# Operands of the fp32r matmuls moved by 32 bytes in SBUF, with padded weight buffers

## The chip, the cores and the metric

The kernel runs on one core of one Trainium2 chip. The metric is the device time of one execution in microseconds (us). A matmul has a stationary operand, which a weight load brings into TensorE (PE) ahead of it, and a moving operand, which streams past it column by column; both are read from SBUF.

## The reference

One layer of a hybrid trunk over 256 frames of width 2048, in float32. All heavy work is two products with large weights:

```python
h = rmsnorm(x, norm_w)
proj = h @ w_in                      # (256, 2048) @ (2048, 13344)
z, xbc, dt_raw, q, k, v, g = jnp.split(proj, IN_SPLITS, axis=-1)
# state-space group: conv, SiLU, chunked scan, gate, group norm    -> y_ssd (256, 2048)
# stick-breaking attention, 16 heads of 128, gate                  -> y_sba (256, 2048)
mix = jnp.concatenate([y_ssd, y_sba], axis=-1)
return x + mix @ w_out               # (256, 4096) @ (4096, 2048), then a final rmsnorm
```

## The kernel before, in words

Both products run in fp32r, with each factor cut into a high and a low part, and three of the four part products are kept. Activations are cut once: `hT` holds the input's high and low parts (128 partitions, 16 slices k of the depth, 2 parts, 256 frames), and `mix_s_hi`, `mix_s_lo`, `mix_a_hi`, `mix_a_lo` hold those of the two head groups. Weights stream through: `load` (L208) brings 1 MB into one of four `raw` buffers, and `cut` (L210) makes the parts `hi` (ScalarE, L225) and `lo` (VectorE, L228) of half of that, in buffers of 1,024 columns, three of each.

The weights' columns are worked off in blocks, one after another, by `run_blocks`, in an order written out by hand. There are two kinds:

- "feat" blocks, 37 of them with 256 columns (in the tiles c, b, z, x, q, k, g): the weights are stationary, the activations move. For each of 16 slices k, L262 issues two matmuls in which all 512 columns of `hT[:, k]` (high and low part, which lie side by side) move past `hi`, and L265 two in which the 256 columns of its high part move past `lo`.
- "tok" blocks (z0 to z2, c1, v0 to v3, o0 to o3): the activations are stationary, 128 frames at a time, and 512 columns of `hi` or `lo` move (288 in c1). For each slice and each half of the frames there are three matmuls, L256 to L258; o3's last step takes 256 columns at a time (L239 to L241).

By the code that is 37 x 64 = 2,368 fp32r matmuls in feat blocks, half with 512 and half with 256 columns, and 288 + 96 + 384 + 774 = 1,542 in tok blocks, 3,910 in all. Besides them, transposes (moving operand `ident`) and small float32 products of the scan and the attention are put between the steps of the blocks by queues with costs; each of those float32 products runs as two passes in the trace, a transpose as one.

SBUF is laid out by pools in the order of their creation: `const`, `stream` (raw, hi, lo), `mixp` (xt and mix_s_hi, sz and mix_s_lo), then `qv`, `half`, `hpool` (hT), `ssd`, and later `mixa`, `att` and, for o3, `fin` (further hi and lo buffers). Places are multiples of 32 bytes. Before the change, raw, hi, lo, xt, sz, mix, the tok tiles of q, k, v and g, hT and nearly all of the rest start 32 bytes past a multiple of 64 bytes in their partition: the first hi buffer at byte 57,632, hT at 133,408, mix_s_hi at 82,208. All slices that the fp32r matmuls take are multiples of 512 bytes (1,152 in c1) from there. `ident`, `ones` and `tri`, the first tiles of `const`, start at multiples of 64.

Of the kernel before, what the change touches and what calls it, by code (L numbers as in the profile page):

```python
# [9 lines left out]
F32 = mybir.dt.float32  # L10
F32R = mybir.dt.float32r
# [7 lines left out]
P = 128  # L19
# [33 lines left out]
def hybrid_kernel(ctx, tc, x, norm_w, w_in, conv_w, conv_b, dt_bias, a_log, d_skip,  # L53
# [9 lines left out]
    const = ctx.enter_context(tc.tile_pool(name="const", bufs=1))  # L63
# [7 lines left out]
        return ps_s.tile([P, 512], F32, tag="s", name=name)  # L71


    ident = const.tile([P, P], F32, name="ident")
    make_identity(nc, ident)
    ones = const.tile([P, P], F32, name="ones")
# [133 lines left out]
    def cut(b, s, each=None):  # L210

        n, name, width = b["n"], f"{b['name']}_{s}", KS[b["kind"]]
        k, kc = s * width, KC[b["kind"]]
        src = raws[b["name"], k // kc][:, k % kc:k % kc + width, :]
        pool, bufs = (b["pool"](), 3) if b["pool"] is not None and s % 2 else (stream, 3)

        def part(which):
            t = pool.tile([P, 1024], F32R, tag=which, name=f"{which}_{name}", bufs=bufs)
            return t[:, 0:width * n].rearrange("p (k n) -> p k n", k=width)
        hi, lo = part("hi"), part("lo")  # L220
        parts = [slice(0, width)] if each is None else [slice(i, i + 1) for i in range(width)]
        for ks in parts:
            if each is not None:
                each(ks.start)
            ins = ac.copy(hi[:, ks, :], src[:, ks, :])  # L225
            if b is blocks[0]:
                last_cut[0] = ins.ins
            ve.tensor_tensor(out=lo[:, ks, :], in0=src[:, ks, :], in1=hi[:, ks, :].bitcast(F32), op=ALU.subtract)  # L228
        cuts[b["name"], s] = hi, lo
# [820 lines left out]
```

## Time and profile before

| what | value |
|---|---|
| median of 3 runs | 829.27 us (829.16 to 829.34) |
| the profiled execution | 829.74 us |
| its span, first to last instruction | 828.0 us |
| PE busy | 814.8 us, 98% |
| VectorE busy, ScalarE busy | 529.8 us (64%), 453.8 us (55%) |
| granted TensorE clock, mean | 0.998 |

Matmuls are pipelined, so a matmul's own duration in the trace overlaps its successor's. What a matmul costs in a stream is the distance from its start to the start of the next one. The timeline view gives starts to 0.01 us, and the distance is taken over many of them.

### The profile page before, as it was taken

The numbers are of one execution on the slowest core, as the hardware profiler recorded it, in microseconds if no ns is written. First come the engines' busy times: TensorE is split into PE (matmuls) and PEld (weight loads), VectorE is DVE, ScalarE is ACT, GpSimd is POOL, SyncE is SP. The second block draws the span as 40 slices with busy tenths as digits, with TensorE's granted clock in tenths as the row PEclk, the third lists the DMA queues.
The fourth block names the chain that finished last, engine by engine and source line by source line (L and its number), as shares of the span: only waits on it lengthen the run. The fifth ranks groups of instructions, "written<-read, shape, count | busy, mean of one in ns | idle before, by whom it ended". The sixth has DMA issues, their size and how long they took to land.

```text
span 828.0 us, 11381 instructions
## 1 busy us (share of the span) xinstructions
PE 814.8 (98%) x4411; PEld 697.5 (84%) x4411; DVE 529.8 (64%) x754; ACT 453.8 (55%) x666; POOL 67.1 (8%) x133
## 2 busy tenths in 40 slices
PE   8999999999999999999999999999999999999995
PEld 6888988888888888888888888888888888888884
DVE  5669596577899868686545654566545655454543
ACT  5766578955797745365445444455444544344433
POOL 0000003000201011022001210022000310000000
PEclk9999999999999999999999999999999999999999
DMA  9854677566667665545566645665465846555712
GB/s 297 289 183 137 193 221 221 179 198 186 200 187 216 196 221 157 171 144 191 156 192 174 187 156 162 197 197 160 153 203 189 320 153 200 181 185 196 254 52 101
DMA packets 117114, 156.34 MB, mean 189 GB/s; under 512 B 3356, under 2 KB 83764, under 8 KB 116676
## 3 DMA queue, kind: packets, MB, share of 16 engines
q1 hardware_dynamic: 115316, 149.29, 57.2%
q0 software_dynamic: 1712, 6.33, 2.3%
q8 instruction: 34, 0.56, 0.3%
q14 instruction: 20, 0.16, 0.1%
q10 hardware_dynamic: 32, 0.01, 0.0%
HBM read 153.48 MB, written 2.13 MB: 188 GB/s over the span
## 4 chain that ended last, share of the span: by engine, by line
PE 97%; DMA 1%; ACT 1%; DVE 1%; SPq 0%; issue 0%; DVEq 0%
PE mm_x L262 7%; PE mm_q L262 7%; PE mm_g L262 7%; PE mm_k L262 7%; PE mm_o L256 7%; PE mm_o L258 7%; PE mm_o L257 7%; PE mm_q L265 4%; PE mm_k L265 4%; PE mm_x L265 4%; PE mm_g L265 4%; PE mm_v L256 4%; PE mm_v L257 3%; PE mm_v L258 3%; PE mm_z L257 3%; PE mm_z L256 3%
## 5 line engine op out<-in xcount | busy, mean ns | idle before, releaser
L228 DVE TENSOR_TENSOR lo_o<-raw_o,hi_o 128x1024 fp32r<-128x1024 f32 x64 | 78.1, 1224 | 74.4 <-ACT hi_o L225 74.4
L225 ACT CAST hi_o<-raw_o 128x1024 fp32r<-128x1024 f32 x64 | 67.1, 1053 | 95.3 <-PE mm_o L258 81.6
L262 PE MATMUL mm_q<-hT,hi_q 128*128 128x512 f32 x256 | 82.5, 403 | 0.0
L262 PE MATMUL mm_k<-hT,hi_k 128*128 128x512 f32 x256 | 81.6, 400 | 0.0
L262 PE MATMUL mm_x<-hT,hi_x 128*128 128x512 f32 x256 | 80.9, 397 | 0.0
L262 PE MATMUL mm_g<-hT,hi_g 128*128 128x512 f32 x256 | 80.6, 396 | 0.0
L228 DVE TENSOR_TENSOR lo_v<-raw_v,hi_v 128x1024 fp32r<-128x1024 f32 x32 | 39.2, 1225 | 44.2 <-ACT hi_v L225 44.2
L228 DVE TENSOR_TENSOR lo_g<-raw_g,hi_g 128x1024 fp32r<-128x1024 f32 x32 | 39.2, 1225 | 38.1 <-ACT hi_g L225 38.1
L225 ACT CAST hi_v<-raw_v 128x1024 fp32r<-128x1024 f32 x32 | 33.6, 1051 | 47.5 <-PE mm_v L258 27.8
L225 ACT CAST hi_g<-raw_g 128x1024 fp32r<-128x1024 f32 x32 | 33.6, 1051 | 44.6 <-PE mm_g L262 25.9
L265 PEld LDWEIGHTS mm_x<-hT,lo_x 128*128 128x128 f32 x256 | 48.1, 188 | 11.3
L265 PEld LDWEIGHTS mm_k<-hT,lo_k 128*128 128x128 f32 x256 | 48.1, 188 | 11.4
L265 PEld LDWEIGHTS mm_g<-hT,lo_g 128*128 128x128 f32 x256 | 48.1, 188 | 11.3
L265 PEld LDWEIGHTS mm_q<-hT,lo_q 128*128 128x128 f32 x256 | 48.0, 188 | 11.2
L225 ACT CAST hi_q<-raw_q 128x1024 fp32r<-128x1024 f32 x32 | 33.5, 1048 | 39.6 <-PE mm_q L262 18.1
L228 DVE TENSOR_TENSOR lo_k<-raw_k,hi_k 128x1024 fp32r<-128x1024 f32 x32 | 39.7, 1241 | 22.7 <-ACT hi_k L225 22.7
L228 DVE TENSOR_TENSOR lo_x<-raw_x,hi_x 128x1024 fp32r<-128x1024 f32 x32 | 39.8, 1244 | 22.2 <-ACT hi_x L225 17.3
L228 DVE TENSOR_TENSOR lo_q<-raw_q,hi_q 128x1024 fp32r<-128x1024 f32 x32 | 39.1, 1223 | 19.0 <-ACT hi_q L225 18.9
L265 PE MATMUL mm_q<-hT,lo_q 128*128 128x256 f32 x256 | 50.9, 280 | 0.0
L228 DVE TENSOR_TENSOR lo_z<-raw_z,hi_z 128x1024 fp32r<-128x1024 f32 (+1 forms) x34 | 39.3, 1160 | 17.9 <-ACT hi_z L225 17.7
L256 PE MATMUL mm_o<-hi_o,mix_s_hi 128*128 128x512 f32 x128 | 50.6, 395 | 0.0
L265 PE MATMUL mm_k<-hT,lo_k 128*128 128x256 f32 x256 | 50.4, 278 | 0.0
(263 smaller groups left out, 1985.3 us busy)
## 6 DMA issues: line engine op xcount, KB each, us to landing
raw_o<-in_w_out_dram SPq DMA_DIRECT2D x32, 1024.0 KB, 5.2
raw_x<-in_w_in_dram SPq DMA_DIRECT2D x16, 1024.0 KB, 5.3
raw_q<-in_w_in_dram SPq DMA_DIRECT2D x16, 1024.0 KB, 5.3
raw_k<-in_w_in_dram SPq DMA_DIRECT2D x16, 1024.0 KB, 5.3
raw_v<-in_w_in_dram SPq DMA_DIRECT2D x16, 1024.0 KB, 5.0
raw_g<-in_w_in_dram SPq DMA_DIRECT2D x16, 1024.0 KB, 5.3
raw_z<-in_w_in_dram SPq DMA_DIRECT2D x12, 1024.0 KB, 5.3
raw_b<-in_w_in_dram SPq DMA_DIRECT2D x4, 1024.0 KB, 5.5
```

The source lines that it names most:

```text
L225: ins = ac.copy(hi[:, ks, :], src[:, ks, :])
L228: ve.tensor_tensor(out=lo[:, ks, :], in0=src[:, ks, :], in1=hi[:, ks, :].bitcast(F32), op=ALU.subtract)
L256: te.matmul(o, lhsT=ah[:, ts], rhs=hi[:, k2, :], start=first, stop=False)
L257: te.matmul(o, lhsT=ah[:, ts], rhs=lo[:, k2, :], start=False, stop=False)
L258: te.matmul(o, lhsT=al[:, ts], rhs=hi[:, k2, :], start=False, stop=last)
L262: te.matmul(acc[i], lhsT=hi[:, k2, i * P:(i + 1) * P], rhs=hT[:, k, :, :].rearrange("p a s -> p (a s)"), start=first, stop=False, skip_gro ...
L265: te.matmul(acc[i][:, 0:SEQ], lhsT=lo[:, k2, i * P:(i + 1) * P], rhs=hT_hi[:, k, :], start=False, stop=last, skip_group_check=True)
```

## The change

A tile of 8 columns (32 bytes) that nothing uses is put first into `const`, so that everything behind it starts 32 bytes later. The buffers of hi and lo are 1,040 columns wide in place of 1,024, and feat blocks use columns 8 to 1,031 of theirs, tok blocks columns 0 to 1,023 as before.

```diff
+    const.tile([P, 8], F32, name="pad")
     ident = const.tile([P, P], F32, name="ident")
...
         def part(which):
-            t = pool.tile([P, 1024], F32R, tag=which, name=f"{which}_{name}", bufs=bufs)
-            return t[:, 0:width * n].rearrange("p (k n) -> p k n", k=width)
+            t = pool.tile([P, 1040], F32R, tag=which, name=f"{which}_{name}", bufs=bufs)
+            at = 8 if b["kind"] == "feat" else 0
+            return t[:, at:at + width * n].rearrange("p (k n) -> p k n", k=width)
```

Worked out from the sizes, raw, hT, mix and the buffers of hi and lo then start at multiples of 64 bytes (a buffer is 4,160 bytes, 65 x 64), the weights of feat blocks 32 bytes past one, and so do `ident`, `ones` and `tri`. No instruction is added, removed or reordered.

## Rows read from the trace of the kernel before

**Rows 1.** The page: busy time of PE; granted clock over 40 slices.
```profile
PE 814.8 (98%) x4411; PEld 697.5 (84%) x4411; DVE 529.8 (64%) x754; ACT 453.8 (55%) x666; POOL 67.1 (8%) x133
...
PEclk9999999999999999999999999999999999999999
```
**Rows 2.** The page: share of engines in the chain that ended last.
```profile
PE 97%; DMA 1%; ACT 1%; DVE 1%; SPq 0%; issue 0%; DVEq 0%
```
**Rows 3.** Waits of PE: who waited for whom, us in total, times, longest.
```profile
PE warm L319 <- POOL ident masks.py:199: 1.5, 1, 1.5
PE ps_x L403 <- DMA xt<-in_x_dram: 1.2, 2, 0.6
PE ps_q L743 <- DVE ssq L738: 0.9, 1, 0.9
PE ps_w L856 <- issue: 0.8, 1, 0.8
PE mm_z L257 <- DVE lo_z L228: 0.2, 1, 0.2
```
**Rows 4.** Timeline of PE (start, us, instruction), tok block, 512 columns: first, last of 14.
```profile
699.82 0.39 PE L256 MATMUL mm_o<-hi_o,mix_s_hi 128*128 128x512 f32 x1
...
702.99 0.39 PE L258 MATMUL mm_o<-hi_o,mix_s_lo 128*128 128x512 f32 x1
```
**Rows 5.** The same, tok block c1, 288 columns: first and last of 11.
```profile
94.75 0.29 PE L257 MATMUL mm_c<-lo_c,hT 128*128 128x288 f32 x1
...
96.08 0.30 PE L258 MATMUL mm_c<-hi_c,hT 128*128 128x288 f32 x1
```
**Rows 6.** The same, the end of o3, 256 columns: first and last of 12.
```profile
818.14 0.28 PE L239 MATMUL mm_o<-hi_o,mix_a_hi 128*128 128x256 f32 x1
...
819.45 0.28 PE L241 MATMUL mm_o<-hi_o,mix_a_lo 128*128 128x256 f32 x1
```
**Rows 7.** The chain by start and length: feat blocks (24 rows, every second slice), side streams.
```profile
144.78 2.68 PE ps_cb L628 x24
...
153.03 0.47 PE mm_x L262 x2
...
185.07 0.47 PE mm_x L262 x2
186.47 0.87 PE ps_xs L661 x8
...
209.65 0.89 PE ps_yo L709 x8
```
**Rows 8.** Groups of weight loads: shapes, count, busy us, mean ns, idle.
```profile
L265 PEld LDWEIGHTS mm_q<-hT,lo_q 128*128 128x128 f32 x256 | 48.0, 188 | 11.2
...
L429 PEld LDWEIGHTS ps_r<-r_diag,ones 128*128 128x128 f32 x2 | 0.4, 188 | 0.1
```
**Rows 9.** Busy time by stretch: PE, weight loads, VectorE, ScalarE, POOL; clock, DMA.
```profile
100.00:120.00 20.00, 20.00 (x125) 17.98 (x124) 16.94 (x39) 14.77 (x21) 0.00 (x0) 1.00 0.80 250
...
140.00:160.00 20.00, 20.00 (x125) 17.83 (x124) 11.95 (x11) 19.89 (x35) 0.00 (x0) 1.00 0.55 167
```
**Rows 10.** The page: HBM traffic, and rates in 40 slices.
```profile
GB/s 297 289 183 137 193 221 221 179 198 186 200 187 216 196 221 157 171 144 191 156 192 174 187 156 162 197 197 160 153 203 189 320 153 200 181 185 196 254 52 101
...
HBM read 153.48 MB, written 2.13 MB: 188 GB/s over the span
```
**Rows 11.** Timeline of PE: a feat block's first slices, behind a tok block.
```profile
520.83 0.39 PE L258 MATMUL mm_v<-hi_v,hT 128*128 128x512 f32 x1
521.06 0.62 PE L262 MATMUL mm_g<-hT,hi_g 128*128 128x512 f32 x2
521.51 0.40 PE L265 MATMUL mm_g<-hT,lo_g 128*128 128x256 f32 x2
521.74 0.63 PE L262 MATMUL mm_g<-hT,hi_g 128*128 128x512 f32 x2
522.21 0.28 PE L265 MATMUL mm_g<-hT,lo_g 128*128 128x256 f32 x1
```
**Rows 12.** Timeline of all engines at the end of o3's full steps: matmuls and loads.
```profile
812.24 0.39 PE L257 MATMUL mm_o<-lo_o,mix_a_hi 128*128 128x512 f32 x1
812.25 0.19 PEld L258 LDWEIGHTS mm_o<-hi_o,mix_a_lo 128*128 128x128 f32 x1
812.47 0.39 PE L258 MATMUL mm_o<-hi_o,mix_a_lo 128*128 128x512 f32 x1
812.47 0.19 PEld L256 LDWEIGHTS mm_o<-hi_o,mix_a_hi 128*128 128x128 f32 x1
```

## The prediction

> **What bounds the kernel now.** I read the page first: PE is busy 98% of the span at the full granted clock, the 2.4 GHz level [rows 1], and 97% of the chain that ended last is PE [rows 2]. The list of PE's waits then shows that this is no queueing behind somebody else: its waits add up to 4.6 us, nearly all at the start [rows 3]. So the time is the number of matmuls times the distance between their starts, and whatever changes that distance reaches the end in full.
>
> The distances are the core of the case. In a tok block, 14 steps take 702.99 - 699.82 = 3.17 us, 226.4 ns for 512 columns [rows 4]. At 2.4 GHz 512 columns are 213.3 ns, so 13 ns are over. In c1 it is 1.33 us in 10 steps, 133 ns for 288 columns against 120 [rows 5], again 13 over; at the end of o3 1.31 us in 11 steps, 119 ns for 256 columns against 106.7 [rows 6], 12 over. The surplus is thus the same at three widths: each matmul pays it once, not each column. In a feat block a slice of two matmuls with 512 and two with 256 columns takes (185.07 - 153.03) / 46 = 0.6965 us [rows 7], against 640 ns of pure columns: 56 over, 14 for each of four. Over 3,910 fp32r matmuls the surplus is 2,368 x 14.1 + 1,542 x 13 = 53 us, 6% of the time. The change can only work on that sum.
>
> Two more kinds of stream lie beside it, the float32 ones (a product is two passes, a transpose one), where a pass of 128 columns moves at half the rate: 256 cycles, 106.7 ns. The transposes of ps_xs, whose moving operand starts on a whole line, take 0.87 / 8 = 109 ns; ps_cb and ps_yo, whose moving operand starts at 32 bytes, 2.68 / 24 = 111.7 and 0.89 / 8 = 111 [rows 7]. At half rate the surplus is thus only 2.1 to 5 ns, and the smaller value is that of the aligned operand.
>
> **The change part by part.**
>
> *Moving operands.* In feat blocks hT, in tok blocks hi and lo, go from 32 bytes past a line to a line's start. A read of 512 columns that begins in the middle of a line touches 33 lines of 64 bytes, an aligned one 32; with 288 it is 19 against 18, with 256 17 against 16. The difference is one line at every width, like the measured surplus. All fp32r operands of the kernel lie at 32 bytes, so no row has an aligned fp32r matmul. The bounds are these: nothing, if the surplus belongs to the fp32r mode; and 13 - 2.3 = 10.7 ns of a tok matmul, if all goes but the 2.3 ns that the aligned transposes keep (109 - 106.7). Between them lies one line: 16 columns of 4 bytes, 6.7 ns at 2.4 GHz, an estimate. I take this one, since it is what the geometry takes away, and the float32 rows, where an aligned stream is cheaper by 2 to 2.7 ns at half rate, say that something goes and not that everything does.
> For tok blocks that is 1,542 x 6.7 = 10.3 us.
>
> *The feat blocks' 256-column matmuls.* During each the next weights are loaded, 128 columns, still from 32 bytes past a line. In the streams of 128-column passes, one load follows another at 109 to 112 ns [rows 7], which I take as the floor for the distance of two loads. Two 512-column ones take 0.47 us in the chain, rounded to hundredths [rows 7], which leaves between (696.5 - 475) / 2 = 111 and (696.5 - 465) / 2 = 116 ns for one with 256; I take 115, since 106.7 plus the surplus of the other kinds would be still more. So it can fall by 115 - 111.5 = 3.5, not by 6.7. A slice then saves 2 x 6.7 + 2 x 3.5 = 20.4 ns, and 592 slices (37 x 16) save 12.1 us.
>
> *Stationary operands.* In tok blocks the activations, stationary there, move to whole lines. A load from `ones`, which is on a line, takes 188 ns, one of lo_q at 32 bytes also 188 [rows 8]; and beside matmuls of 226 ns a load has time to spare. I cost it at nothing; the bound on both sides is in the rivals.
>
> *Side matmuls.* The pad comes before `ident`, `ones` and `tri`, so the transposes lose their line and the products with CT, cb, k and wT gain one. By the code these are 136 transposes (ps_x, ps_zt, ps_xs, ps_w) and 184 passes; at 2 to 2.7 ns for each [rows 7] that is 0.3 us lost and 0.4 won, nothing on balance.
>
> *The other engines and DMA.* ScalarE and VectorE see all big operands 32 bytes away, and no row has them otherwise. Their slack covers it except in 140 to 160 us, where ScalarE is busy 19.89 of 20 [rows 9]: with a PE 3% faster, up to 0.6 us of the gain could be held back there. HBM delivers 188 GB/s on average and 297 and 320 in its best slices [rows 10]; 3% more is no bound. The buffers take 416 bytes more, nothing is evicted for it, and no queue is reordered.
>
> Sum: 10.3 + 12.1 = 22.4 us. The profiled execution took 829.74, of it 828.0 span and 1.7 around it, which stays; its span falls to 805.6 and its time to 807.3. The median of the runs lies 0.47 below the profiled one, so the forecast is 829.27 - 22.4 = 806.9 us.
>
> [...]
>
> **The rivals.**
>
> 1. *Nothing changes.* The constant 13 ns is what an fp32r matmul costs, wherever its operands lie. For it: the float32 passes hardly have the surplus although most of their operands lie at 32 bytes too, so the mode is what differs most clearly. [...] Time 829.3, at most 0.5 off.
> 2. *All the surplus goes.* Tok 1,542 x 10.7 = 16.5 us; a feat slice falls to 2 x (213.3 + 2.3) + 2 x 111.5 = 654 ns, 592 x 42.5 = 25.2 us. Time 787.6. For it: the surplus is of one piece at all widths.
> 3. *Only the feat blocks gain.* The matmul's read and the weight load beside it start within 0.01 us of each other [rows 12], today at the same half of a line. If the surplus is their collision, what helps is that feat blocks now have weights at 32 and activations at 0, while tok blocks have both at 0, as alike as before. The first slice behind a tok block takes 0.68 us [rows 11], those in the run 0.70 [rows 7]: the streams' phase does matter in feat blocks. Gain 12.1 (as above) to 25.2; time 804 to 817, middle 811.
> 4. *Slower.* The same collision with the other sign: like starts are the good case, since both streams then change lines at once, and unlike ones make every feat matmul lose one line more. Price 2,368 x 6.7 = 15.8 us, time 845. It decides from the point where a feat slice takes longer than 0.6965 us by more than tok matmuls save for it, 10.3 us / 592 = 17 ns. For it: a slice's cost is not fixed (0.68 and 0.70), so it can rise too. Against it: both blocks, with quite different streams, have the same surplus today.
>
> **How the numbers follow.** Forecast 0.37, nothing 0.23, all of it 0.14, only feat 0.11, slower 0.15. About 0.2% (1.7 us) is what a measurement of this kernel can tell from no change. Faster is 0.37 + 0.14 + 0.11 = 0.62, same 0.23, slower 0.15. The range goes from the second rival, with 1 us for what I can't place, 786.5, to the first with its spread and a little more, 831; it leaves out the fourth and a sliver below, some 0.17. The forecast's own range is 800 to 814.
>
> **What would show it.** In the profile after: tok matmuls 220 ns apart instead of 226.4, c1's 126 instead of 133, feat slices 676 ns instead of 696.5, PE still with 97% of the chain. If tok distances stay at 226 and feat slices fall, the third rival holds; if both stay, the first; 216 and 654, the second; feat slices over 700, the fourth. If the distances fall but the time doesn't follow, PE's list of waits must name a new releaser, ScalarE's `hi` between 140 and 160 us first. The prediction is wrong at its root if the surplus has nothing to do with where a read begins.

## The result, and the profile after

The changed kernel takes 836.34 us (835.85 to 836.75), the kernel before 829.16 in the same session: the ratio is 1.0086, with a 95% interval of 1.0075 to 1.0097. It is slower by 7.2 us, where 22.4 us less were forecast, and outside the range (786.5 to 831). The profiled execution took 836.75 us, of it 835.0 span.

The page of the changed kernel, busy time and the chain by engine, to be held against [rows 1, 2]:

```profile
PE 823.8 (99%) x4411; PEld 702.2 (84%) x4411; DVE 530.4 (64%) x754; ACT 453.2 (54%) x666; POOL 67.4 (8%) x133
...
PE 98%; ACT 1%; DVE 1%; issue 0%; DVEq 0%; POOL 0%; POOLq 0%
```

Its list of PE's waits (who waited for whom, us, times, longest), against [rows 3]:

```profile
PE warm L323 <- POOL ident masks.py:199: 1.5, 1, 1.5
PE ps_q L747 <- DVE ssq L742: 1.1, 1, 1.1
PE ps_w L860 <- issue: 0.8, 1, 0.8
```

No new wait has come: 3.4 us in place of 4.6. VectorE and ScalarE are as busy as before, to 0.6 us. The 7 us are in PE's own stream, so the distance between starts is what to look at. The timeline of PE in the changed kernel, in feat blocks (a row is the two matmuls with 512 columns of one slice, and from the first row shown to the last it is 47 slices), then 30 steps in a tok block:

```profile
151.84 0.63 PE L266 MATMUL mm_z<-hT,hi_z 128*128 128x512 f32 x2
...
184.85 0.62 PE L266 MATMUL mm_x<-hT,hi_x 128*128 128x512 f32 x2
...
719.84 0.39 PE L260 MATMUL mm_o<-hi_o,mix_a_hi 128*128 128x512 f32 x1
...
726.75 0.39 PE L260 MATMUL mm_o<-hi_o,mix_a_hi 128*128 128x512 f32 x1
```

A feat slice takes (184.85 - 151.84) / 47 = 0.7023 us, where [rows 7] have 0.6965; a tok matmul 6.91 / 30 = 230.3 ns, where [rows 4] have 226.4. So both kinds of blocks lose. And the stream isn't even any more. These are 16 tok matmuls in a row in the changed kernel, six of them left out:

```profile
708.33 0.39 PE L261 MATMUL mm_o<-lo_o,mix_s_hi 128*128 128x512 f32 x1
708.56 0.39 PE L262 MATMUL mm_o<-hi_o,mix_s_lo 128*128 128x512 f32 x1
708.79 0.39 PE L260 MATMUL mm_o<-hi_o,mix_s_hi 128*128 128x512 f32 x1
709.02 0.39 PE L261 MATMUL mm_o<-lo_o,mix_s_hi 128*128 128x512 f32 x1
...
710.62 0.39 PE L262 MATMUL mm_o<-hi_o,mix_s_lo 128*128 128x512 f32 x1
710.85 0.40 PE L260 MATMUL mm_o<-hi_o,mix_s_hi 128*128 128x512 f32 x1
711.09 0.39 PE L261 MATMUL mm_o<-lo_o,mix_s_hi 128*128 128x512 f32 x1
711.32 0.39 PE L262 MATMUL mm_o<-hi_o,mix_s_lo 128*128 128x512 f32 x1
711.55 0.39 PE L260 MATMUL mm_o<-hi_o,mix_s_hi 128*128 128x512 f32 x1
711.78 0.40 PE L261 MATMUL mm_o<-lo_o,mix_s_hi 128*128 128x512 f32 x1
```

Up to 710.85, eleven steps take 229 ns each on average; there the next buffers of hi and lo begin, the first step is 0.24 us, and the four shown take 232.5 ns each. The tempo changes with the buffer that is read. That was the clue: buffers of 1,040 columns follow each other at 4,160 bytes. Before, every operand of an fp32r matmul outside c1 lay at the same place modulo 512, so that the distance between the moving operand and the weights (whatever is stationary: in tok blocks the activations), in bytes, was always a multiple of 512. (In c1 a slice of the weights is 1,152 bytes, so that every second slice lies 128 bytes further on.) Now it goes through all multiples of 64, with the 32 bytes of the skipped columns on top in feat blocks. A matmul and the load of the next weights start within 0.01 us of each other [rows 12]. In all the kernels below in which the distance is fixed, the next weights lie at the same place modulo 512 as the present ones, so it is one distance for both.

### The profile page after: what moved, and what is told of

It reads as the page before. It is cut to its first block, busy times and chain, and to the rows that moved or that the text cites. A ratio compares the mean times of both kernels' runs of the same rounds, so it can differ in the third digit from the quotient of the medians.

```text
span 835.0 us, 11381 instructions
## 1 busy us (share of the span) xinstructions
PE 823.8 (99%) x4411; PEld 702.2 (84%) x4411; DVE 530.4 (64%) x754; ACT 453.2 (54%) x666; POOL 67.4 (8%) x133
## 4 chain that ended last, share of the span: by engine, by line
PE 98%; ACT 1%; DVE 1%; issue 0%; DVEq 0%; POOL 0%; POOLq 0%
PE mm_q L266 7%; PE mm_x L266 7%; PE mm_g L266 7%; PE mm_k L266 7%; PE mm_o L261 7%; PE mm_o L260 7%; PE mm_o L262 7%; PE mm_q L269 4%; PE mm_g L269 4%; PE mm_x L269 4%; PE mm_k L269 4%; PE mm_v L260 4%; PE mm_v L261 3%; PE mm_v L262 3%; PE mm_z L261 3%; PE mm_z L260 3%
## 5 line engine op out<-in xcount | busy, mean ns | idle before, releaser
L269 PE MATMUL mm_g<-hT,lo_g 128*128 128x256 f32 x256 | 51.1, 281 | 0.0
L269 PE MATMUL mm_x<-hT,lo_x 128*128 128x256 f32 x256 | 51.1, 281 | 0.0
```

The costliest lines, as they stand in the source:

```text
L269: te.matmul(acc[i][:, 0:SEQ], lhsT=lo[:, k2, i * P:(i + 1) * P], rhs=hT_hi[:, k, :], start=False, stop=last, skip_group_check=True)
```

## The experiments

From here on "distance" is the address of the moving operand less that of the stationary one, modulo 256 (why 256 shows below). The table has, for each run, the ratio to the kernel before with its interval, and two means over all starts of the profiled execution: the step from one tok matmul with 512 columns to the next, and a feat slice as the sum of the mean steps of its four matmuls (steps over 260 ns, where other work lies between, left out).

| kernel | distance tok / feat | tok ns | slice ns | us | ratio |
|---|---|---|---|---|---|
| before | 0 / 0 | 227.2 | 697.2 | 829.2 to 829.4 | 1 |
| changed | mixed / mixed | 230.4 | 702.4 | 836.34 | 1.0086 (1.0075 to 1.0097) |
| e1_pad_only | 0 / 0 | 227.3 | 697.2 | 829.19 | 0.9998 (0.9990 to 1.0007) |
| e2_width_only | mixed / mixed | 230.4 | 700.6 | 835.01 | 1.0068 (1.0055 to 1.0080) |
| e14_no_offset | mixed / mixed | 230.4 | 700.5 | 834.66 | 1.0071 (1.0057 to 1.0085) |
| e3_acts_32 | 224 / 32 | 232.9 | 695.0 | 835.31 | 1.0070 (1.0057 to 1.0082) |
| e4_acts_128 | 128 / 128 | 232.5 | 697.8 | 836.70 | 1.0087 (1.0072 to 1.0103) |
| e5_repair | 0 / 224 | 227.3 | 702.9 | 832.45 | 1.0040 (1.0027 to 1.0052) |
| e6_feat_32 | 0 / 32 | 227.3 | 697.3 | 829.27 | 1.0001 (0.9993 to 1.0010) |
| e7_feat448_tok256 | 0 / 192 | 227.3 | 694.3 | 827.88 | 0.9984 (0.9975 to 0.9993) |
| e8_feat256_tok32 | 32 / 0 | 233.2 | 697.3 | 836.96 | 1.0095 (1.0079 to 1.0110) |
| e10_feat64_tok192 | 192 / 64 | 233.3 | 692.0 | 834.30 | 1.0062 (1.0049 to 1.0074) |
| e11_feat160_tok64 | 64 / 160 | 229.1 | 703.3 | 835.13 | 1.0071 (1.0058 to 1.0084) |
| e12_feat96_tok96 | 96 / 96 | 233.4 | 702.8 | 839.86 | 1.0128 (1.0114 to 1.0141) |
| e13_feat64_tok0 | 0 / 64 | 227.3 | 691.7 | 826.32 | 0.9967 (0.9954 to 0.9979) |

In e3_acts_32 and e4_acts_128 every second step of o3 takes its weights from `fin`, which lies behind the pad like the activations, so that these stay at distance 0. Without o3 their tok means are 233.2 and 232.8 ns.

**Lines or distance.** Four kernels take the change apart. The first has the pad alone:

```diff
+    const.tile([P, 8], F32, name="pad")
     ident = const.tile([P, P], F32, name="ident")
```

> Only the pad of the change: all operands of the fp32r matmuls start on whole 64-byte lines, buffers stay 1,024 columns wide, feat blocks use columns 0 to 1,023. Every moving operand keeps its distance to the weights loaded beside it, a multiple of 512 bytes as before. Theory 'distance' (the changed kernel is slower because the distances between the two reads are no longer multiples of 512 bytes): as before, 829 +- 1 us, tok distance 226.7 ns, feat slice 697 ns. Theory 'start' (where in a line a read begins decides, and a line's start is the worse place): about 836 us, tok 230 ns, feat slice 702 ns. Forecast of the prediction (a line's start is the better place): 807 us, tok 220 ns.

The second has the width alone:

```diff
-            t = pool.tile([P, 1024], F32R, tag=which, name=f"{which}_{name}", bufs=bufs)
+            t = pool.tile([P, 1040], F32R, tag=which, name=f"{which}_{name}", bufs=bufs)
```

> Only the width of the change: buffers of hi and lo 1,040 columns wide, no pad, no columns skipped. All operands still start 32 bytes past a line, as before, but the buffers follow each other at 4,160 bytes, so the distances between moving operand and weights take all multiples of 64 bytes. Theory 'distance': slower, 834 to 838 us, tok distance 230 ns in place of 226.7, feat slice 700 to 703 ns. Theory 'start': as before, 829 +- 1 us.

The third and the fourth put a pad into the pool that follows the weights, so that activations and mix move and the weights don't (8 columns in the third, 32 in the fourth):

```diff
+    mixp.tile([P, 8], F32, name="pad")
     xt = [mixp.tile([P, NB, 512], F32, tag="mix0", name=f"xt_{i}", bufs=4) for i in range(KIN // 4)]
```

> Activations and mix alone 32 bytes later, on whole lines; weights stay 32 bytes past a line and 1,024 columns wide. Feat blocks then read at the places of the changed kernel (activations on a line, weights at 32), but always at a distance of 32 bytes modulo 512; tok blocks move from 32 bytes past a line, with weights loaded from a line's start, distance 480 modulo 512. Theory 'distance': both kinds of blocks change, by how much is open: tok between 225 and 234 ns, feat slice between 686 and 710, nothing tied to the line. Theory 'start': feat slices as in the changed kernel, 702 ns, tok as before, 226.7, together 832 us.

> Activations and mix alone 128 bytes later: all starts stay 32 bytes past a 64-byte line, and the distance between the two reads is 128 (feat) and 384 (tok) modulo 512 throughout. Theory 'distance': tok 231 ns (in the changed kernel matmuls at distance 128 modulo 256 are 231.5 apart), 833 to 838 us. Theory 'start': as before, 829 +- 1 us, tok 226.7 ns, feat slice 697 ns.

The timeline of PE with the pad alone: the same stretch of feat blocks, then 30 steps of a tok block.

```profile
151.95 0.63 PE L263 MATMUL mm_z<-hT,hi_z 128*128 128x512 f32 x2
...
184.69 0.63 PE L263 MATMUL mm_x<-hT,hi_x 128*128 128x512 f32 x2
...
720.00 0.39 PE L257 MATMUL mm_o<-hi_o,mix_a_hi 128*128 128x512 f32 x1
...
726.80 0.39 PE L257 MATMUL mm_o<-hi_o,mix_a_hi 128*128 128x512 f32 x1
```

That is 32.74 / 47 = 0.6966 us and 6.80 / 30 = 226.7 ns, the numbers of the kernel before, with every fp32r operand on a whole line. At an equal distance (0 here) the start in a line did nothing, 829.19 us against 829.32. The fourth kernel never leaves the place of 32 bytes past a line and is as slow as the changed one. Its timeline, 29 steps of a tok block:

```profile
719.88 0.39 PE L258 MATMUL mm_o<-hi_o,mix_a_lo 128*128 128x512 f32 x1
...
726.64 0.40 PE L257 MATMUL mm_o<-lo_o,mix_a_hi 128*128 128x512 f32 x1
```

6.76 / 29 = 233 ns at distance 128. Block o3 of the same kernel holds both cases side by side: there 12 matmuls that read from `fin`, at distance 0, take turns with 12 that read from `stream`, at 128. From the first to the second row shown are 10 steps of the latter, from the third to the fourth 8 of the former:

```profile
788.88 0.40 PE L257 MATMUL mm_o<-lo_o,mix_s_hi 128*128 128x512 f32 x1
...
791.22 0.39 PE L258 MATMUL mm_o<-hi_o,mix_s_lo 128*128 128x512 f32 x1
791.45 0.39 PE L256 MATMUL mm_o<-hi_o,mix_s_hi 128*128 128x512 f32 x1
...
793.26 0.39 PE L258 MATMUL mm_o<-hi_o,mix_s_lo 128*128 128x512 f32 x1
```

2.34 / 10 = 234 ns and 1.81 / 8 = 226 ns, in one block, by one and the same lines of code. And the width alone, on unchanged lines, has 5.7 of the 7.2 us, with the 230.4 ns that were expected of it. The theory "start" falls with these three, and the forecast's with it. In the third run, activations 32 bytes later cost a tok matmul 6 ns outside o3 (distance 224) and give a feat slice 2.2 (distance 32). In the third and fourth kernels the weights' buffers in `stream` stay where they were, so the places at which ScalarE and VectorE cut the weights are not what slows the tok matmuls.

The kernel before holds a small case of its own. In c1, where every second slice lies 128 bytes further on, the matmuls with 288 columns follow each other at 131.8 ns in the slices at distance 0 and at 133.8 ns in the others (means over 48 and 47 starts of its trace). With the activations 128 bytes later, in the fourth kernel, the two change places: 133.6 and 131.8.

**The repair.** If the distance is the cause, the changed kernel with buffers that follow each other at a multiple of 512 must lose nothing in tok blocks. 1,152 columns are 4,608 bytes; room for them comes from letting `nw_rows`, `par` and `sn_rows` share two places and putting `r_bc` and four small tiles of `softplus_dt` into the pool `ssd`. This form carries the following runs too, each with its own two columns at which a buffer's use begins (feat, tok):

```diff
-            t = pool.tile([P, 1040], F32R, tag=which, name=f"{which}_{name}", bufs=bufs)
+            t = pool.tile([P, 1152], F32R, tag=which, name=f"{which}_{name}", bufs=bufs)
             at = 8 if b["kind"] == "feat" else 0
```

> The changed kernel (pad, feat weights 32 bytes past a line, everything else on lines) with buffers 1,152 columns wide in place of 1,040, so that they follow each other at 4,608 bytes, a multiple of 512; to make room, some small tiles of parameters share places or lie in another pool. Every distance between a moving operand and the weights loaded beside it is then fixed: 0 modulo 512 in tok blocks, 480 in feat blocks. Theory 'distance': the loss goes, tok 227 ns apart again, 826 to 831 us (feat slice 694 to 701 ns, its price at 480 is not yet measured). Rival 'wide buffers' (whatever spreads the buffers costs time, by their places and not by the distance): 834 to 837 us, tok 230 ns.

Tok is back at 227.3, and the time at 832.45, above the 826 to 831 expected: feat slices stay at 702.9. They have a fixed distance now, 224, and it is a bad one. So the expectation of the total missed, for the price of a distance that hadn't been measured, while the tok part came out. The timeline, feat then tok (30 steps):

```profile
152.17 0.63 PE L265 MATMUL mm_z<-hT,hi_z 128*128 128x512 f32 x2
...
185.19 0.63 PE L265 MATMUL mm_x<-hT,hi_x 128*128 128x512 f32 x2
...
719.90 0.39 PE L260 MATMUL mm_o<-lo_o,mix_a_hi 128*128 128x512 f32 x1
...
726.70 0.39 PE L260 MATMUL mm_o<-lo_o,mix_a_hi 128*128 128x512 f32 x1
```

33.02 / 47 = 0.7026 us, 6.80 / 30 = 226.7 ns. The remaining 3.2 us are 592 x 5.7 ns = 3.4 us of feat slices. The rival "wide buffers" falls: they are wider still, and tok blocks lose nothing. The new places of the small tiles cost nothing that shows either: the next kernel has them too and takes 829.27 us.

**The other side and the period.** Columns 120 and 0; 16 and 64; 64 and 8:

> As the one before, but feat blocks use columns 120 to 1,143 of their buffers: distance 32 modulo 512 in feat blocks, 0 in tok blocks, all tok operands on lines. Theory 'distance': feat slice 695 ns as with the activations 32 bytes later (697.2 in the kernel before), tok 227: 592 x 2.2 ns = 1.3 us faster than the kernel before, 828.0 us. Rival 'wide buffers': 834 to 837 us.

> As the two before, with feat blocks at columns 16 to 1,039 and tok blocks at 64 to 1,087: distance 448 modulo 512 in feat blocks, 256 in tok blocks, all on lines. Theory 'distance' with period 256: tok 227 ns; with period 512: tok about 230 ns, as matmuls at distance 256 modulo 512 had in the changed kernel (229.8). Feat slice between 695 and 703. Total 828 to 837 us. A theory that knows only lines expects 829.

> As the three before, with feat blocks at columns 64 to 1,087 and tok blocks at 8 to 1,031: distance 256 modulo 512 in feat blocks (all on lines) and 32 in tok blocks (moving operand 32 bytes past a line, weights loaded from a line). Theory 'distance': tok about 233 ns (232.9 was measured at 480, the same 32 bytes with the other sign), feat slice 697 if the period is 256, else up to 703; 838 us and more. A theory that knows only lines expects the tok blocks to be as in the kernel before, 829.

In the second of them tok blocks stand at 256 modulo 512 and take 227.3 ns, as at 0; in the third feat blocks do and take 697.3 per slice. So 256 bytes more change nothing at this place, while 128 do (c1 agrees: 133.8 ns at 128 modulo 512, 133.6 at 384). The table therefore counts modulo 256; at the other distances the period wasn't tested. Tok steps of the second kernel, 30 of them:

```profile
719.95 0.39 PE L260 MATMUL mm_o<-lo_o,mix_a_hi 128*128 128x512 f32 x1
...
726.75 0.39 PE L260 MATMUL mm_o<-lo_o,mix_a_hi 128*128 128x512 f32 x1
```

6.80 / 30 = 226.7 ns, as at distance 0. This is the third one's timeline, feat and 29 steps of tok:

```profile
151.84 0.63 PE L265 MATMUL mm_z<-hT,hi_z 128*128 128x512 f32 x2
...
184.58 0.63 PE L265 MATMUL mm_x<-hT,hi_x 128*128 128x512 f32 x2
...
720.00 0.39 PE L261 MATMUL mm_o<-hi_o,mix_a_lo 128*128 128x512 f32 x1
...
726.77 0.40 PE L260 MATMUL mm_o<-lo_o,mix_a_hi 128*128 128x512 f32 x1
```

32.74 / 47 = 0.6966 us as before the change, and 6.77 / 29 = 233.4 ns at distance 32: 837 us, 1 us under what was expected. The second came out just beyond its bounds, at 827.88 us and 694.3 ns per slice. The first missed by 1.3 us: at distance 32 feat slices were expected at 695.0 and took 697.3 on average. Its trace shows two beats at the same distance. Stretches of 693 to 694 ns and others of 706 to 707 alternate, each behind one to three slices in which it settles, and a beat holds until other work interrupts the stream:

```profile
151.88 0.62 PE L265 MATMUL mm_z<-hT,hi_z 128*128 128x512 f32 x2
...
170.60 0.62 PE L265 MATMUL mm_x<-hT,hi_x 128*128 128x512 f32 x2
...
615.89 0.63 PE L265 MATMUL mm_g<-hT,hi_g 128*128 128x512 f32 x2
616.59 0.63 PE L265 MATMUL mm_g<-hT,hi_g 128*128 128x512 f32 x2
617.30 0.63 PE L265 MATMUL mm_g<-hT,hi_g 128*128 128x512 f32 x2
```

The first stretch has 27 slices of 18.72 / 27 = 0.693 us, the second is shown with two of 0.705, and over all its 31 slices has 0.7067. The third kernel of the first four, at the same distance, was mostly in the shorter beat. What picks the beat isn't settled. The second kernel here, at feat distance 192, is the first that is faster than the kernel before, 0.9984 (0.9975 to 0.9993).

**The rest of the circle.** Columns 112 and 48; 88 and 16; 104 and 24:

> Buffers 1,152 columns wide, feat blocks at columns 112 to 1,135, tok blocks at 48 to 1,071: distance 64 modulo 256 in feat and 192 in tok blocks, all starts on lines. Theory 'distance': tok between 228 and 231 ns (matmuls at 192 modulo 256 were 229.6 apart in the changed kernel, where distances were mixed), 832 to 836 us with feat slices between 694 and 700. Theory that knows only lines: 829.

> As the one before with columns 88 to 1,111 and 16 to 1,039: distance 160 modulo 256 in feat and 64 in tok blocks. Theory 'distance': tok about 230.5 ns (230.6 in the changed kernel), feat slices between 694 (measured at 192) and 698 (at 128): 831 to 836 us.

> As the two before with columns 104 to 1,127 and 24 to 1,047: distance 96 modulo 256 in both kinds of blocks. Theory 'distance': tok between 230 and 233 ns (neighbours 64 and 128 had 230.6 and 232.5), feat slices 695 to 698 (neighbours 32 and 128): 833 to 838 us.

All three were slower, the first two within the times expected, the last 1.9 us over; but prices of the single kinds missed. Tok at 192 takes 233.3 and not the 229.6 read out of the changed kernel, where distances change from buffer to buffer. Feat at 160 takes 703.3 and not 694 to 698, at 96 702.8 and not 695 to 698: these had been taken from the neighbouring distances, and the price doesn't run smoothly between them. A tok matmul at distance 0 takes 227.3, at 64 229.1, at 32, 96, 128, 192 and 224 it is 232.8 to 233.4 (the values of e3 and e4 taken without o3); 160 wasn't run. A feat slice goes up and down with the distance: 697, 695 or 697, 692, 703, 698, 703, 694, 703 at 0, 32, 64, 96, 128, 160, 192 and 224.

The first of these kernels also shows that the price at a distance isn't the same at every width. At 192 the tok matmuls with 512 columns are slow, and those with 256 at the end of o3 are faster than before, 114 ns against 119 (first and last of 12):

```profile
823.30 0.28 PE L242 MATMUL mm_o<-hi_o,mix_a_hi 128*128 128x256 f32 x1
...
824.55 0.28 PE L244 MATMUL mm_o<-hi_o,mix_a_lo 128*128 128x256 f32 x1
```

1.25 / 11 = 114 ns, where [rows 6] have 119: 7 ns over the columns in place of 12, while the matmuls with 512 have 20 in place of 14 (a column counted at 0.417 ns, an estimate from [rows 4, 5]: 226.4 - 133 = 93.4 ns for 224 columns more).

**Is the constant 13 ns what the load takes?** If the surplus of [rows 4 to 6] were stolen by the reads of the weight load, half a load should steal half. In blocks o1 and o2, all slices but the first and the last:

```diff
                     o = acc[i][:, 0:n]
+                    if b["name"] in ("o1", "o2") and not first and not last:
+                        ts, o = slice(i * P, i * P + 64), acc[i][0:64, 0:n]
```

> The kernel before, but in blocks o1 and o2 the matmuls of all slices except the first and the last take only 64 of the 128 stationary columns (frames 64 to 127 and 192 to 255 of these output columns are then left without most of their sum). 360 matmuls with 512 moving columns then stand beside a weight load half as long. Theory 'collision' (the constant 13 ns that an fp32r matmul pays over its columns is what the load's reads take from the moving read): about half goes, these matmuls 220 ns apart in place of 226.7, 2.4 us less, 826.9 us. Rival 'mode' (the 13 ns belong to the matmul whatever is loaded beside it): 226.7 ns, 829.2 us.

The load is shorter, 134 ns in place of 188, and the matmuls beside it aren't. A group of loads (shapes, count, busy us, mean ns, idle):

```profile
L259 PEld LDWEIGHTS mm_o<-lo_o,mix_s_hi 128*64 128x64 f32 x60 | 8.1, 134 | 5.6
```

Eight steps of the timeline beside such loads:

```profile
700.14 0.40 PE L258 MATMUL mm_o<-hi_o,mix_s_hi 128*64 128x512 f32 x1
...
701.98 0.39 PE L260 MATMUL mm_o<-hi_o,mix_s_lo 128*64 128x512 f32 x1
```

1.84 / 8 = 230 ns, 3 more than with the whole load, and 830.38 us, ratio 1.0011 (1.0002 to 1.0021). Neither theory has it: the surplus didn't shrink, so it doesn't go with the amount that is loaded; nor is it fixed whatever lies beside, since it rose. The edit also halves the stationary columns that the matmul itself uses, and the two aren't told apart. Where the 13 ns come from stays open.

**Do the kinds add?** The best distance of each kind in one kernel, columns 112 and 0:

> Buffers 1,152 columns wide, feat blocks at columns 112 to 1,135, tok blocks at 0 to 1,023, all starts on lines: the best distance found for each kind, 64 modulo 256 in feat and 0 in tok blocks. Theory 'distance' (the kinds add, each with its own price by distance): feat slices 692.0 ns, tok 227.3; 592 x 5.2 ns = 3.1 us less than the kernel before, 826.1 us. If the prices depend on something else that went along in the runs so far (the other kind's places), the sum fails: 829 or more.

826.32 us, 0.2 from the sum that was written down, and 0.9967 (0.9954 to 0.9979) of the kernel before: the fastest of all. Its timeline has 48 slices and 30 tok steps:

```profile
152.06 0.62 PE L265 MATMUL mm_z<-hT,hi_z 128*128 128x512 f32 x2
...
185.17 0.62 PE L265 MATMUL mm_x<-hT,hi_x 128*128 128x512 f32 x2
...
719.93 0.39 PE L259 MATMUL mm_o<-hi_o,mix_a_hi 128*128 128x512 f32 x1
...
726.73 0.39 PE L259 MATMUL mm_o<-hi_o,mix_a_hi 128*128 128x512 f32 x1
```

33.11 / 48 = 0.690 us, 6.80 / 30 = 226.7 ns.

**The share of the skipped columns.** The changed kernel without them:

```diff
-            at = 8 if b["kind"] == "feat" else 0
+            at = 0
```

> The changed kernel without its third part: pad and width 1,040, but feat blocks at columns 0 to 1,023 as tok blocks. All starts on lines, distances all multiples of 64 bytes. Theory 'distance': as with the width alone, 835.0 us, tok 230.4, feat slice 700.6 ns; the 8 columns then account for the last 1.3 us of the changed kernel's loss. Theory that lines matter: faster than the width alone.

834.66 us, tok 230.4, slice 700.5: the width alone with the pad beside it. The changed kernel's loss is therefore nothing from the pad and 5.5 to 5.7 us from the width. What is left, 1.5 to 1.7 us, goes to the 8 columns that feat blocks skip; this share is less sure, since the intervals of the two ratios overlap (1.0075 to 1.0097 and 1.0057 to 1.0085) and the slices account for 592 x 1.9 ns = 1.1 us of it.

## Why the prediction was wrong

- *What bounds the kernel.* This held. PE's distance between starts sets the time, and what the change did to it reached the end. The measured 7.2 us stand against 1,434 x 3.2 ns = 4.6 us of tok matmuls with 512 columns and 592 x 5.2 ns = 3.1 us of feat slices, 7.7 us in all; PE's waits are 1.2 us shorter, so that some 0.7 us has no place in this sum.
- *Moving operands,* the step that failed. The term was 10.3 us for tok and most of 12.1 us for feat, one line of 16 columns per matmul. The pad alone puts every read on a whole line, and its time is the same as before within the noise (0.1 us of 829 less, 0.9990 to 1.0007). The term is nothing. That 64 bytes are a unit of reading stood in no row: it was taken from the step of the change. That the surplus was the same at three widths made it look like a line too many; it fits any cost per matmul, and the two float32 streams that differed by 2 to 2.7 ns were no proof for a line. The clock under the surplus is to be read from [rows 4, 5], not from [rows 1], which have the granted share alone: 93.4 ns for 224 columns more are 0.417 ns a column, 2.4 columns a nanosecond. The means over the whole trace of before at distance 0, 227.2 and 131.8 ns, give 0.426, and so 218 ns for 512 columns where 213 were counted: every figure "over the columns", here and above, is an estimate. So is the 106.7 ns of a float32 pass: [rows 7] have 109 to 112 ns for its 128 columns, 0.85 to 0.87 each, about twice an fp32r column. Nor is the surplus "14 for each of four" in a feat slice: its matmuls with 512 columns take 233 ns, 20 over, those with 256 take 115 to 116, 8 to 10 over, and the prediction's own 0.47 us for two and 115 for one say as much.
- *The width of the buffers,* the step that wasn't there. The prediction has one sentence on it, that 416 bytes more evict nothing. It is the part with the price, 5.5 to 5.7 of the 7.2 us: at 4,160 bytes from buffer to buffer the distance to the activations is another in every buffer. The addresses were at hand, and written side by side they show that all fp32r operands outside c1 were alike modulo 512 before and aren't afterwards. What it would cost, the trace of before could hardly say: all that it shows of it are the 2 ns between the slices of c1.
- *The feat blocks' floor* at 111.5 ns for a 256-column matmul was never tested, since nothing shortened these to it: in the changed kernel they are at 118 to 119, before at 115 to 116. All that feat slices lose in the changed kernel is lost there: the steps of their matmuls with 512 columns stay at 233 ns.
- *Stationary operands at nothing.* Right as a matter of lines (the pad alone), wrong as a matter of distance. *Side matmuls, other engines, DMA:* nothing showed; ScalarE is busy 19.9 of 20 us in its worst stretch before and after, and PE didn't wait for it.
- *The rivals.* The first, that a line does nothing, is true of the lines and had the wrong end, because the change does more than move lines. The second, that all the surplus goes, would have tok matmuls at 216 ns; none of these kernels has them under 227. The fourth, slower, had half of it: two operands whose relative place has a price, with unlike places the worse ones on the whole (tok 229.1 to 233.4 ns against 227.3; a feat slice up to 703.3 against 697.2, though 691.7 at 64). Its sign, feat slices over 700 ns, came (702.4). But it looked for the unlike places in the 32 bytes within a line and not in the width, sized the feat blocks at 15.8 us, where they cost 3.1, and had no loss in tok blocks, where 4.6 are lost. The third had the relative place as well, with the sign turned round.

What stays open: by what mechanism the distance sets the price; where the 13 ns at distance 0 come from; whether the distance that counts is that to the weights loaded beside a matmul or that to its own, which lie alike in all the kernels with a fixed distance; and what chooses between two beats at the same distance.

## What to carry to other kernels

Where a stream of matmuls is bound by PE itself, write the places of the moving and the stationary operands side by side, modulo 256 bytes (here 0 and 256 cost the same, 227.3 ns), before anything changes a buffer's size: padding a rotating buffer made the distance change from buffer to buffer, which cost 5.5 to 5.7 us, where the alignment it was meant for gave 0.1, within the noise. A part of a change that moves no work, such as a wider tile, still has to be costed by everything that its addresses touch. The prices here are of fp32r matmuls and of one kernel; another needs its own run. And prices read out of a stream in which cases are mixed were off by up to 3.7 ns a matmul (229.6 read, 233.3 run); runs that hold one case throughout gave prices whose sum came out to 0.2 us, though even they differed by 2.3 ns a slice (695.0 and 697.3) where the stream has two beats.

## What the runs showed of the hardware

- In a stream of fp32r matmuls the distance between starts went with the address of the moving operand less that of the stationary one: 227.3 ns (distance 0) to 233.4 ns (96) for 512 moving columns with activations stationary, 691.7 to 703.3 ns for a slice of two matmuls with 512 and two with 256 columns (64 and 160). 256 bytes more changed nothing: 227.3 ns and 697.3 at 256 against 227.2 and 697.2 at 0, and in c1 133.6 at 384 against 133.8 at 128.
- Moving both operands from 32 bytes past a multiple of 64 to the multiple, at equal distance (0), changed nothing: 829.19 us against 829.32.
- No distance that was run removed the surplus over the columns, by the estimate of 0.417 ns a column from [rows 4, 5]: at best 14 ns of 227.3 for a tok matmul with 512, 51 of 691.7 for a feat slice of four. It isn't one constant: at distance 192 tok matmuls with 256 columns have 7 ns and those with 512 have 20. Matmuls that use, and load, half the stationary columns (loads of 134 ns in place of 188) had no less of it, 230 ns in place of 227.
- Two steady beats of 693 and 707 ns per slice were seen at one and the same distance.
